# A hybrid encoder on one core: decays of the score matrices moved to later convolutions, a triangular inversion kept on VectorE, two more dense steps before its merge

## The chip, the cores and the metric

The kernel runs on one core of one Trainium2 chip. The metric is the device time of one launch in microseconds; the number given for a kernel is the median of its runs. Lower is better.

## The reference

Two encoder layers over a sequence of 1024 tokens of width 1024, all in float32, and a final RMSNorm. In each layer x is normed, projected by one matrix of 3376 columns, and the columns go to three groups of heads: gated linear attention (GLA), a gated DeltaNet, and cross-attention into 256 memory tokens. The outputs are normed, gated, concatenated and projected back. The change touches the gated DeltaNet and the dense projection alone. For the DeltaNet, q, k and v pass a centred depthwise convolution of 5 taps and SiLU; q and k are L2-normalised. Then, per head, direction and chunk of 64 tokens:

```python
gc = jnp.cumsum(g, axis=-1)
diff = gc[..., :, None] - gc[..., None, :]
decay = jnp.where(incl, jnp.exp(jnp.where(incl, diff, 0.0)), 0.0)
kk = jnp.einsum('bhncd,bhnsd->bhncs', k, k)
a_strict = jnp.where(strict, kk * decay * beta[..., :, None], 0.0)
t_mat = a_strict + jnp.eye(c, dtype=jnp.float32)
sol = lax.linalg.triangular_solve(t_mat, rhs, left_side=True, lower=True, unit_diagonal=True)
qk = jnp.where(incl, jnp.einsum('bhncd,bhnsd->bhncs', q, k) * decay, 0.0)
```

The decays depend on the gates alone, not on q, k or v. The unit triangular matrices of 64 x 64 are inverted once, before the scan over the chunks.

## The kernel before, in words

**Stages.** A layer is `phase_norm` (norm, transposes, the first 432 projection columns, gates), `phase_proj` (the convolutions, L2 norms, decays, score matrices, inversion) and `phase_mix` (the scan over chunks as a chain of blocks, with GLA, attention, gating and the output projection filled in between). TensorE's instructions stay in the order in which the program issues them (`pin`, L92, and `mat`, L97). The instructions of the other engines are placed on each engine by a planner that simulates the program (L1656), apart from those that are pinned too.

**The dense projection.** `dense_gen` (L449) makes the 23 remaining column tiles of 128, each in two halves of 512 tokens. A half is four units of six matmuls of 128x512 (three for each of two k, since float32 is split in a high and a low part). One `next` makes one unit. `pull(ns)` (L475) takes units until ns is used up at 1290 a unit, and `upto(n)` (L482) takes them until n tiles are whole. There are 184 units in a layer, so a unit pulled early is one less later. At the end of a half a sink (L487, L519) copies PSUM out on ScalarE; there are two PSUM buffers (`mm`, L171), so the half after the next waits for it. The weights of the next tile are split at its first unit: `wh` on ScalarE and `wl` on GpSimd (L178).

**The convolutions.** `conv_sink` (L519) for a tile: ScalarE writes `pad` and the middle tap into `acc` (L531, L532); after the second half VectorE adds four taps (L535, 128x1024 each); ScalarE makes the sigmoid in three passes and GpSimd multiplies (L538). `conv_t` (L542) later transposes the result on TensorE. The order of the tiles is three of k, three of v, three of q (L436).

**The decays.** `decays` (L648) is a generator. Its first step builds a mask and issues eight loads of N. Each later step treats one of four heads on 128x1024 elements: a subtraction on GpSimd (L671, pinned), a minimum on VectorE (L672), an exponential on ScalarE (L673). `phase_proj` calls a step after each of the three key convolutions (L599) and after the second and third value convolution (L611); the fifth call finds the generator at its end. The result is first read in `phase_a` (L676), after the query convolutions.

**The inversion.** `invert` (L701) transposes blocks of 32x32 into U (L713) and makes the inverse X column step by column step: for j from 31 down to 1 a product into `tmp` and a subtraction from X. Columns 0 to 29 (`CUT` = 30) are made on VectorE (L732 to L738). The last two columns, in X2, are made by 62 instructions on GpSimd (L724 to L731), and ScalarE copies them into X (L739). Then VectorE transposes X into FT and M for both directions (L745, L747). The merge of the 32-blocks into 64-blocks is matmuls of 32x32 on TensorE (L765, L778). The generator yields how much dense work is to be pulled: 20000 (`INV0`, 16 units), eight single units among the matmuls of the memory's key and value projection (`kv`, L1414 to L1430), and 6000 (`INV`, five units) ahead of the merge.

**The filler.** What is left of the dense units is taken in `phase_mix` by `filler` (L829): 3, 24 and 5 units, then the rest between the steps of the mixers (L860 to L872), and after it the loads and splits of the output weights.

Of the kernel before, what the change touches and what calls it, by code (L numbers as in the profile page):

```python
# [8 lines left out]
F32 = mybir.dt.float32  # L9
# [4 lines left out]
ALU = mybir.AluOpType  # L14
# [3 lines left out]
P = 128  # L18
# [19 lines left out]
LAG = 2  # L38
PRE_D = 24
INV0 = 20000  # L40
INV = 6000
XPOS = 5
DC0 = 0
CUT = 30
MIX0 = 5
MIXU = 21
MIXN = 16
# [12 lines left out]
class Kern:  # L60
# [510 lines left out]
    def phase_proj(self, l):  # L571
        nc = self.nc
        GC, self.closeGC = self.pool("GC", side=self.sb)
        self.ST, self.closeST = self.pool("ST", side=self.sb)
        ST = self.ST
        KTp, closeKT = self.pool("KT", side=self.sb)
        closePX = self.psum(tr=2, cp=2, kv=2)
        dec = self.decays(GC)
        N = next(dec)

        self.kv_d = self.DR.tile([2, NT, P, 384], F32, tag="kvd", name="kv_d")
        self.qd_d = self.DR.tile([2, HD, 4, T], F32, tag="qdd", name="qd_d")
        kT = [KTp.tile([HD, T], F32, name=f"kT{h}") for h in range(4)]
        qT = KTp.tile([HD, 4, T], F32, name="qT")
        tok = lambda: ST.tile([P, NT, 384], F32, tag="tok", name="tok", bufs=1)

        def v_out(i):
            v = ST.tile([P, NT, P], F32, tag="v_t", name="v_t", bufs=1)
            self.conv_t(6 + i, v)
            nc.sync.dma_start(self.kv_d[1, :, :, i * 128:i * 128 + 128].rearrange("t p c -> p t c"), v)  # L590
        U = 1290
        k_tok = tok()
        self.upto(2)
        for i in range(3):

            self.upto(3 + i)
            self.pull(DK * U)
            self.conv_t(3 + i, k_tok[:, :, i * 128:i * 128 + 128])
            if i >= DC0:  # L599
                next(dec, None)  # L600
        self.l2norm(ST, k_tok, 1.0)
        nc.sync.dma_start(self.kv_d[0].rearrange("t p c -> p t c"), k_tok)
        self.upto(6)
        self.pull(DV * U)
        v_out(0)
        q_tok = None
        for i in range(2):
            self.upto(7 + i)
            self.pull(DV * U)
            v_out(1 + i)  # L610
            next(dec, None)  # L611
            if i == 0:
                for h in range(4):
                    self.back_t(k_tok, h, kT[h])
                    self.pull(U)
                q_tok = tok()
        for i in range(3):
            self.upto(9 + i)
            self.pull(DQ * U)
            self.conv_t(i, q_tok[:, :, i * 128:i * 128 + 128])  # L620
        for _ in dec:
            pass
        self.l2norm(ST, q_tok, HD ** -0.5)
        self.pull(8 * U)
        for h in range(4):
            self.back_t(q_tok, h, qT[:, h, :])
            for d in range(2):
                row = ST.tile([P, T], F32, tag="acc", name="row", bufs=3)[0:HD]
                nc.sync.dma_start(row.rearrange("p (t c) -> p t c", t=NT),
                                  self.row_d[:, d * 4 + h].unsqueeze(0).to_broadcast([HD, NT, P]))  # L630
                self.ptt(row, row, qT[:, h, :], ALU.mult)
                nc.sync.dma_start(self.qd_d[d, :, h], row)
            self.pull(U)
        for _ in self.phase_a(N, kT, qT, KTp):
            self.pull(U)
        closeKT()
        self.closeST()
        GQ, self.closeGQ = self.pool("GQ", side=self.sa)
        R, closeR = self.pool("GR", side=self.sa)
        self.gla_gate_ops(l, GQ, R)  # L640
        closeR()
        SX, self.closeSX = self.pool("SX", side=self.sb)
        for g in self.invert(l, N, SX):
            self.pull(g)
        closePX()
# [55 lines left out]
    def invert(self, l, N, SX):  # L701

        nc = self.nc

        U = SX.tile([P, 2, 32, 32], F32, name="U")
# [8 lines left out]
        X = SX.tile([P, 2, 32, 32], F32, name="X")  # L714
        nc.gpsimd.memset(X, 0.0)
        Xf = X.rearrange("p b s c -> p b (s c)")
        nc.gpsimd.memset(Xf[:, :, 0:1024:33], 1.0)

        n2 = 32 - CUT
        X2 = SX.tile([P, 2, 32, n2], F32, name="X2")  # L720
        nc.gpsimd.memset(X2, 0.0)
        for c in range(n2):
            nc.gpsimd.memset(X2[:, :, CUT + c, c:c + 1], 1.0)
        for j in range(31, 0, -1):  # L724
            c0 = max(j - CUT, 0)
            w = n2 - c0
            tmp = SX.tile([P, 2, 32, n2], F32, tag="tmp2", name="tmp2", bufs=1)
            tv = tmp[:, :, 0:j, 0:w]
            sh = [P, 2, j, w]
            self.ptt(tv, U[:, :, 0:j, j:j + 1].to_broadcast(sh), X2[:, :, j:j + 1, c0:].to_broadcast(sh), ALU.mult)  # L730
            self.ptt(X2[:, :, 0:j, c0:], X2[:, :, 0:j, c0:], tv, ALU.subtract)  # L731
        for j in range(CUT - 1, 0, -1):  # L732
            w = CUT - j
            tmp = SX.tile([P, 2, 256], F32, tag="tmp", name="tmp", bufs=1)
            tv = tmp[:, :, 0:j * w].rearrange("p b (s c) -> p b s c", s=j)
            sh = [P, 2, j, w]
            self.tt(tv, U[:, :, 0:j, j:j + 1].to_broadcast(sh), X[:, :, j:j + 1, j:CUT].to_broadcast(sh), ALU.mult)
            self.tt(X[:, :, 0:j, j:CUT], X[:, :, 0:j, j:CUT], tv, ALU.subtract)  # L738
        self.act(X[:, :, :, CUT:], X2)  # L739

        FT = [SX.tile([P, 4, NT, 32], F32, name=f"FT{d}") for d in range(2)]
        fl = lambda v: v.rearrange("p h t c -> p (h t) c")
# [9 lines left out]
        for c in kv:  # L752
            yield c
        yield INV
        for g in range(2):
# [904 lines left out]
```

## Time and profile before

| | us |
|---|---|
| median of three runs (1391.15 to 1397.26) | 1391.71 |
| the profiled execution's own time | 1387.57 |
| its span from first to last instruction | 1385.8 |

The mean granted TensorE clock of the profiled execution is 0.965 of full speed. 1.77 us of its time lie around the span. Windows and timelines are in microseconds from the start of the span. PE is TensorE's matmuls, DVE VectorE, ACT ScalarE, POOL GpSimd. A matmul's duration overlaps the next one's, so starts are compared, not durations. The name behind `<-` in square brackets is what ended the idle time before the instruction. A line can be a helper's: L84 is any ScalarE activation, L87 a VectorE and L90 a GpSimd two-input operation, L98 a matmul.

### The profile page before, as it was taken

What the parts mean: (1) busy time and instruction counts of PE and PEld (TensorE: products, weight loads), DVE (VectorE), ACT (ScalarE), POOL (GpSimd) and SP (SyncE); (2) the same over time, 40 slices, a digit from 0 to 9 for tenths busy, and PEclk for the clock granted to TensorE, in tenths of its full rate; (3) what the DMA queues carried; (4) which work ended last, traced back from release to release, by engine and by line L of the source; (5) the groups of instructions that cost most, each with busy time, mean ns of one, the idle gap of its engine ahead of it and who ended that gap; (6) DMA issues with size and microseconds to landing.
All of it is one profiled execution on the core that took longest, in us unless ns stands there. A gap on an engine that the chain in (4) does not pass through costs nothing. (4 is left out here: it accounts for less than half of the span.)

```text
span 1385.8 us, 24239 instructions
## 1 busy us (share of the span) xinstructions
PE 1260.7 (91%) x9482; PEld 1047.5 (76%) x9482; DVE 814.8 (59%) x1163; ACT 655.5 (47%) x1373; POOL 549.6 (40%) x579
## 2 busy tenths in 40 slices
PE   6998799987999988999999988996978998999997
PEld 5986688776777777887788766884767787778886
DVE  5336855498377557356272578455865784564553
ACT  5335564162766655233262545531637675543432
POOL 4026434576534544211310454444854445432111
PEclk9999999999999999999999999998999999999999
DMA  7161234752686865244652413257427776642532
GB/s 223 57 134 35 74 91 130 245 157 69 187 242 197 236 192 144 81 145 125 188 169 66 107 46 106 61 158 221 136 66 225 210 229 203 205 130 80 161 103 106
DMA packets 247857, 198.99 MB, mean 144 GB/s; under 512 B 68032, under 2 KB 215936, under 8 KB 247744
## 3 DMA queue, kind: packets, MB, share of 16 engines
q1 hardware_dynamic: 245584, 189.59, 47.2%
q10 hardware_dynamic: 2016, 7.34, 1.5%
q8 instruction: 75, 1.23, 0.4%
q0 software_dynamic: 144, 0.52, 0.1%
q14 instruction: 38, 0.31, 0.1%
HBM read 138.82 MB, written 58.59 MB: 142 GB/s over the span
## 5 line engine op out<-in xcount | busy, mean ns | idle before, releaser
L98 PE MATMUL mm<-Hh,wh 128*128 128x512 f32 x736 | 311.8, 424 | 31.7 <-ACT acc L84 15.9
L98 PE MATMUL mm<-Hh,wl 128*128 128x512 f32 x736 | 295.9, 402 | 0.0
L98 PE MATMUL mm<-Hl,wh 128*128 128x512 f32 x736 | 295.6, 402 | 0.0
L90 POOL TENSOR_TENSOR wl<-wr,wh 128x1024 fp32r<-128x1024 f32 x46 | 119.4, 2596 | 211.0 <-ACT wh L84 188.3
L98 PEld LDWEIGHTS mm<-Hh,wh 128*128 128x128 f32 x736 | 143.5, 195 | 66.7 <-ACT acc L84 19.3
L535 DVE SCALAR_TENSOR_TENSOR acc<-pad,convw,acc 128x1024 f32<-128x1024 f32 x72 | 139.9, 1943 | 66.4 <-ACT acc L84 63.8
L98 PEld LDWEIGHTS mm<-Hh,wl 128*128 128x128 f32 x736 | 143.2, 195 | 32.3
L98 PE MATMUL mm<-wo,oh 128*128 128x512 f32 x512 | 167.1, 407 | 0.2 <-DVE xr L87 0.2
L98 PEld LDWEIGHTS mm<-Hl,wh 128*128 128x128 f32 x736 | 144.2, 196 | 26.0
L90 POOL TENSOR_TENSOR ol<-z,oh 128x512 fp32r<-128x512 f32 x32 | 41.2, 1286 | 163.6 <-ACT oh L84 161.4
L98 PEld LDWEIGHTS mm<-wo,oh 128*128 128x128 f32 x512 | 90.3, 189 | 17.8 <-issue 0.8
L98 PE MATMUL mm<-wo,ol 128*128 128x512 f32 x256 | 101.2, 395 | 0.0
L90 POOL TENSOR_TENSOR S<-S,dec 96x384 f32<-96x384 f32 x56 | 55.5, 991 | 87.4 <-DVE S L87 66.9
L90 POOL TENSOR_TENSOR acc<-acc,pad 128x1024 f32<-128x1024 f32 x18 | 45.6, 2531 | 107.8 <-ACT pad L84 107.8
L84 ACT ACTIVATE wh<-wr 128x1024 fp32r<-128x1024 f32 x46 | 48.4, 1053 | 74.8 <-PE mm L98 66.2
L98 PEld LDWEIGHTS cp<-S,wq 96*128 96x128 f32 x480 | 62.7, 197 | 14.9 <-ACT oa L84 6.4
L98 PE MATMUL cp<-S,wq 96*128 96x96 f32 x480 | 65.1, 280 | 9.2 <-ACT oa L84 5.5
L84 ACT ACTIVATE oh<-z 128x512 fp32r<-128x512 f32 x32 | 20.2, 632 | 80.4 <-DVE z L87 80.3
L87 DVE TENSOR_TENSOR vn<-u,cp 64x384 f32<-64x384 f32 x60 | 33.0, 550 | 40.9 <-PE cp L98 33.4
L98 PEld LDWEIGHTS mm<-wo,ol 128*128 128x128 f32 x256 | 48.1, 188 | 11.5
L90 POOL TENSOR_TENSOR sp<-sp,sg 128x512 f32<-128x512 f32 x32 | 45.3, 1417 | 28.8 <-ACT sg L84 17.6
L90 POOL TENSOR_TENSOR row<-row,qT 96x1024 f32<-96x1024 f32 x16 | 38.0, 2383 | 44.0 <-DMA row<-row_d 29.3
(311 smaller groups left out, 2652.1 us busy)
## 6 DMA issues: line engine op xcount, KB each, us to landing
wr<-in_w_in_dram SPq DMA_DIRECT2D x46, 512.0 KB, 4.0
kv<-kv_d SPq DMA_DIRECT2D x32, 384.0 KB, 4.4
zT<-sp SPq DMA_DIRECT2D x32, 256.0 KB, 2.4
ge_d<-qe SPq DMA_DIRECT2D x32, 256.0 KB, 3.7
wor<-in_w_out_dram SPq DMA_DIRECT2D x16, 512.0 KB, 4.6
gqk<-ge_d SPq DMA_DIRECT2D x16, 512.0 KB, 4.0
z<-zT SPq DMA_DIRECT2D x16, 512.0 KB, 4.5
row<-row_d SPq DMA_DIRECT2D x16, 384.0 KB, 6.3
```

Of the source, the lines that this page charges most:

```text
L84: return self.nc.scalar.activation(out, in_, func, **kw)
L87: return self.nc.vector.tensor_tensor(out, a, b, op=op)
L90: return self.nc.gpsimd.tensor_tensor(out, a, b, op=op)
L98: return self.pin(self.nc.tensor.matmul(*args, **kw))
L535: nc.vector.scalar_tensor_tensor(acc, pad[:, j:j + T], self.convw[:, f, j:j + 1], acc, op0=ALU.mult, op1=ALU.add)
```

## The change

The decay steps are no longer called after the key convolutions. They are called after the second and third value convolution (heads 0 and 1) and after the first two query convolutions (heads 2 and 3; the last call ends the generator). The first step with its eight loads stays where it is. In the inversion all 32 columns are made on VectorE, in 62 instructions in place of 58; X2, its memsets, the 62 GpSimd instructions and ScalarE's copy go. `INV` is 9000, seven units in place of five.

```diff
-INV = 6000
+INV = 9000
 XPOS = 5
-DC0 = 0
-CUT = 30
...
             self.conv_t(3 + i, k_tok[:, :, i * 128:i * 128 + 128])
-            if i >= DC0:
-                next(dec, None)
...
             self.conv_t(i, q_tok[:, :, i * 128:i * 128 + 128])
-        for _ in dec:
-            pass
+            next(dec, None)
...
-        n2 = 32 - CUT
-        X2 = SX.tile([P, 2, 32, n2], F32, name="X2")
-        nc.gpsimd.memset(X2, 0.0)
-        for c in range(n2):
-            nc.gpsimd.memset(X2[:, :, CUT + c, c:c + 1], 1.0)
         for j in range(31, 0, -1):
-            c0 = max(j - CUT, 0)
-            w = n2 - c0
-            tmp = SX.tile([P, 2, 32, n2], F32, tag="tmp2", name="tmp2", bufs=1)
-            tv = tmp[:, :, 0:j, 0:w]
-            sh = [P, 2, j, w]
-            self.ptt(tv, U[:, :, 0:j, j:j + 1].to_broadcast(sh), X2[:, :, j:j + 1, c0:].to_broadcast(sh), ALU.mult)
-            self.ptt(X2[:, :, 0:j, c0:], X2[:, :, 0:j, c0:], tv, ALU.subtract)
-        for j in range(CUT - 1, 0, -1):
-            w = CUT - j
+            w = 32 - j
...
-            self.tt(tv, U[:, :, 0:j, j:j + 1].to_broadcast(sh), X[:, :, j:j + 1, j:CUT].to_broadcast(sh), ALU.mult)
-            self.tt(X[:, :, 0:j, j:CUT], X[:, :, 0:j, j:CUT], tv, ALU.subtract)
-        self.act(X[:, :, :, CUT:], X2)
+            self.tt(tv, U[:, :, 0:j, j:j + 1].to_broadcast(sh), X[:, :, j:j + 1, j:].to_broadcast(sh), ALU.mult)
+            self.tt(X[:, :, 0:j, j:], X[:, :, 0:j, j:], tv, ALU.subtract)
```

## Rows read from the trace of the kernel before

**Rows 1.** Page, part 1: busy us, share of the span, instructions.
```profile
PE 1260.7 (91%) x9482; PEld 1047.5 (76%) x9482; DVE 814.8 (59%) x1163; ACT 655.5 (47%) x1373; POOL 549.6 (40%) x579
```

**Rows 2.** Waits of PE, whole span: us in total, times, longest.
```profile
PE mm L98 <- ACT acc L84: 15.9, 8, 3.5
```

**Rows 3.** Windows, busy us of each engine: value to query convolutions; second layer's mix.
```profile
180.00:240.00 60.00, 60.00 (x300) 50.21 (x299) 34.76 (x29) 31.93 (x49) 23.33 (x15) 1.00 0.36 95
...
1050.00:1240.00 190.00, 175.04 (x1530) 148.18 (x1529) 120.94 (x214) 115.58 (x261) 83.94 (x84) 0.96 0.70 203
```

**Rows 4.** Timeline of PE, first layer's convolutions: start, us, instruction [idle before].
```profile
117.44 0.50 PE L98 MATMUL mm<-Hh,wh 128*128 128x512 f32 x1 [1.54 <-ACT acc L84]
...
133.06 0.80 PE L98 MATMUL mm<-Hh,wh 128*128 128x512 f32 x1 [3.50 <-ACT acc L84]
...
139.70 0.39 PE L98 MATMUL mm<-Hh,wl 128*128 128x512 f32 x1
...
223.38 1.03 PE L101 MATMUL tr<-ident,acc 128*128 128x128 f32 x8
```

**Rows 5.** Timeline of DVE, first layer's convolutions: the four taps.
```profile
117.42 8.87 DVE L535 SCALAR_TENSOR_TENSOR acc<-pad,convw,acc 128x1024 f32<-128x1024 f32 x4 [3.97 <-ACT acc L84]
...
148.42 5.75 DVE L535 SCALAR_TENSOR_TENSOR acc<-pad,convw,acc 128x1024 f32<-128x1024 f32 x2 [1.05 <-ACT acc L84]
...
159.34 1.27 DVE L535 SCALAR_TENSOR_TENSOR acc<-pad,convw,acc 128x1024 f32<-128x1024 f32 x1
...
195.66 7.50 DVE L535 SCALAR_TENSOR_TENSOR acc<-pad,convw,acc 128x1024 f32<-128x1024 f32 x4 [0.43 <-ACT acc L84]
...
208.71 7.50 DVE L535 SCALAR_TENSOR_TENSOR acc<-pad,convw,acc 128x1024 f32<-128x1024 f32 x4 [4.94 <-ACT acc L84]
```

**Rows 6.** Timeline of POOL, first layer's convolutions.
```profile
117.28 2.41 POOL L90 TENSOR_TENSOR wl<-wr,wh 128x1024 fp32r<-128x1024 f32 x1
...
119.71 2.86 POOL L90 TENSOR_TENSOR N<-N,gB 128x1024 f32<-128x1024 f32 x1
...
219.79 2.40 POOL L90 TENSOR_TENSOR acc<-acc,pad 128x1024 f32<-128x1024 f32 x1 [7.38 <-ACT pad L84]
```

**Rows 7.** Timeline of ACT, first layer's convolutions.
```profile
128.54 1.04 ACT L84 ACTIVATE N<-N 128x1024 f32<-128x1024 f32 x1
```

**Rows 8.** Windows of tile X, first layer's inversion: DVE, ACT, POOL busy (count).
```profile
283.80:328.80 45.00, 38.36 (x59) 0.33 (x1) 27.51 (x62) 0.96 0.35 109
```

**Rows 9.** Timeline of DVE, first layer's inversion.
```profile
299.78 2.66 DVE L87 TENSOR_TENSOR X<-X,tmp 128x400 f32<-128x400 f32 x1
...
305.85 1.57 DVE L87 TENSOR_TENSOR X<-X,tmp 128x442 f32<-128x442 f32 x1
...
309.52 0.63 DVE L87 TENSOR_TENSOR X<-X,tmp 128x450 f32<-128x450 f32 x1
...
325.27 0.22 DVE L87 TENSOR_TENSOR X<-X,tmp 128x58 f32<-128x58 f32 x1
328.74 1.97 DVE L745 STREAM_TRANSPOSE FT<-X 128x1024 f32<-128x1024 f32 x1 [3.25 <-ACT X L84]
```

**Rows 10.** Timeline of POOL, first layer's inversion.
```profile
299.28 2.73 POOL L90 TENSOR_TENSOR wl<-wr,wh 128x1024 fp32r<-128x1024 f32 x1
...
334.64 2.37 POOL L90 TENSOR_TENSOR wl<-wr,wh 128x1024 fp32r<-128x1024 f32 x1
```

**Rows 11.** Timeline of ACT, first layer's inversion.
```profile
328.38 0.33 ACT L84 ACTIVATE X<-X 128x128 f32<-128x128 f32 x1 [15.84 <-POOL X L90]
```

**Rows 12.** Timeline of PE, first layer's inversion.
```profile
322.01 0.59 PE L98 MATMUL mm<-Hh,wh 128*128 128x512 f32 x1
...
328.82 0.39 PE L98 MATMUL mm<-Hh,wl 128*128 128x512 f32 x1
331.21 0.50 PE L98 MATMUL mm<-Hh,wh 128*128 128x512 f32 x1 [2.00 <-ACT sg L84]
...
338.55 1.92 PE L98 MATMUL cp<-FT,N 32*32 32x32 f32 x124 [5.50 <-DVE FT L745]
```

## The prediction, made before the change was run

> **What bounds the kernel now.** I read the page's busy times first: TensorE is busy for 91% of the span, 125 us are not [rows 1]. Its matmuls stay in program order, so each of these gaps moves all that comes after it. The list of TensorE's waits then says which gaps the change can reach. The longest in total is for ScalarE to empty a PSUM buffer in the convolutions, 15.9 us in eight waits [rows 2]; the longest in the inversion is the merge's for VectorE's transpose FT, 5.50 in the first layer [rows 12]. The table of windows says where there is room: in the later convolutions of the first layer TensorE is busy for all 60.00 us, with VectorE at 34.76 and GpSimd at 23.33 [rows 3]. Last come the timelines of the two places, the convolutions [rows 4 to 7] and the inversion [rows 9 to 12]. The second layer repeats the first there, so I price one layer and double it.
>
> **Decays leave the key convolutions.** Per layer three heads move: 0, 1 and 2, which after the change stand behind later convolutions as heads 1, 2 and 3. The fourth stays at the second value convolution. What moves is a GpSimd subtraction of 2.86 us, a VectorE minimum, a ScalarE exponential of 1.04 us [rows 6, 7] and no DMA: the eight loads are issued by the first step, which stays, so SP's queue sees nothing. On GpSimd a subtraction passes the convolutions' products and the weight splits between its old place and its new one.
> A convolution is a loop: its four taps on VectorE, the sigmoid on ScalarE, then ScalarE empties the next half, and only then do the next taps start. Without a decay the loop takes 208.71 - 195.66 = 13.05 us. With decays the second and third starts lie at 117.42 and, after two loops, 148.42, so 15.5 us a loop [rows 5]. I see two causes: the taps take 8.87 us in place of 7.50, as they meet a subtraction besides a weight split [rows 5, 6], so 1.37; and the exponential stands on ScalarE ahead of the emptying, 1.04 [rows 7]. The sum is 2.4 a head, which fits.
> Taken out, the start at 117.42 comes 1.54 earlier, for as long as TensorE waited there [rows 4], at 115.9, and two loops of 13.05 later stands 142.0 in place of 148.42. **Gain: 6.4 us** a layer. TensorE, whose work in a loop is eight dense units and a group of transposes (8 x 1.41, worked out below, and 1.03 [rows 4]: 12.3 us), still waits in each loop, but less than the 3.50 of the row at 133.06 [rows 4].
>
> **Decays arrive in the later convolutions.** There the same three heads make the loops late by at most 3 x 2.4 = 7.2 us, and by the key convolutions' own measure 6.4. Two meet in one loop, behind the last value and the first query convolution. Behind GpSimd's subtractions its products and weight splits queue; behind the exponentials ScalarE's emptying of PSUM, for which TensorE waits. The place where it shows last is the transposes of the last query convolution: its GpSimd product ends at 219.79 + 2.40 = 222.19, TensorE takes it at 223.38 [rows 4, 6], so 1.2 us of lateness are covered. No dense work stands behind them that could go first. The cost of a wait there lies between 0 (the planner puts the pieces into the idle time of rows 3) and 7.2 - 1.2 = 6.0. I take 6.4 - 1.2 = 5.2, from the nearest row, the same instructions in the same kind of loop.
> After a wait of this size the clock is low for a while: behind the 3.50 at 133.06 the granted clock falls, and 18 dense matmuls start over 6.64 us, while 30 at the full clock start over 6.81 [rows 4, 12]. That is 6.64 - 17 x 0.235 = 2.6 us, and I add it. In the key convolutions that loss was hidden in the loop's 15.5 us, so it is not gained there. **Net of the decays: -6.4 + 5.2 + 2.6 = +1.4** a layer, between -6.4 and +2.2.
>
> **The inversion, on VectorE alone.** Instructions without company take 0.22 us for 58 elements and 0.63 for 450 [rows 9], so 0.16 us and 1.05 ns an element. Before, 58 of them have 17980 elements, 28.1 us. After, 62 have 21824: 32.8 us and 0.1 for the gaps, **+4.8**. Busy in the row are 38.36 - 0.06 of the first transpose = 38.3 [rows 8]; 10.2 more than 28.1. Two of the instructions meet a weight split (299.78: 2.66 in place of 0.58, under the split from 299.28 [rows 9, 10]) and five a sink's product (305.85: 1.57 in place of 0.62 [rows 9]): 2 x 2.1 + 5 x 0.95 = 9.0. The remaining 1.1 or so comes from the company of the two columns' instructions. That goes: **-1.1**. So does the wait of 3.25 for ScalarE's copy [rows 9]: **-3.25**. X is ready 0.4 us later than before.
> But ScalarE's copy, which stood 15.84 us in front of ScalarE's other work [rows 11], held back the emptying of the `kv` buffers, the next `wh` and with it the split at 334.64 [rows 10], which ran under the transposes, where it cost nothing. Without the copy this split and one sink's product come some ten microseconds earlier, behind the last `kv` matmuls at 322 [rows 12], inside VectorE's longer chain: 2.1 as at 299.78 and about 1 more. X is ready at 328.74 + 3.5 = 332.2, and the merge's FT 3.5 later than 338.55. The stall of 2.00 on `sg` [rows 12] goes, since ScalarE is free, but TensorE then only waits longer for FT: 8 units behind the last `kv` matmuls, from 322.01 at 6 x 0.235 = 1.41 each, end at 333.3, and FT comes at 342. The two units more are 2.8 us that the filler has no longer to do; in the mix TensorE is busy for 175 of 190 us [rows 3], so I count all of it. For a wait of 8.7 us in one piece the clock costs a little more than after 5.50 and 2.00: I add 0.4, from a bound of 0 and the 2.6 above. **Net: +3.5 - 2.8 + 0.4 = +1.1** a layer, between 0.4 - 2.8 = -2.4 (no new meeting with GpSimd) and +3.5 + 2.6 = +6.1 (the mix, bound by its chain there, gives nothing back).
> The memsets of X2 and the 62 GpSimd instructions lie beside other work and count nothing more: GpSimd's own end was seen only through the copy.
>
> **A rule weighed.** The 62 GpSimd instructions are busy for 27.51 us beside VectorE's, and yet cost VectorE 1.1 us [rows 8, 9]; a 2.7 us split costs it 2.1 [rows 9, 10]. The Trainium skill, page "SBUF — State Buffer", section "Who interferes with whom", says that a VectorE instruction with two SBUF inputs and a GpSimd instruction that reads SBUF exclude each other for the whole instruction, and that the order of issue decides who waits. By it the short ones would make VectorE wait as well as the long, up to 27.51 us in all, and the chain would come out much shorter without them; the row says they do not, the long ones agree, and the sum goes by the rows.
>
> **Sum.** 2 x (1.4 + 1.1) = +5.0 us. The profiled execution would go from 1387.57 (span 1385.8 and 1.77 around it) to 1392.6. That execution is 4.1 under the median of the three runs, 1391.71, so the median becomes **1396.7 us**. A measurement of this kernel tells 0.5%, 7.0 us, from no change; this is 0.36%.
>
> **Rivals.** *The later convolutions hide the decays* (faster). For it: 60.00 of 60.00 us of TensorE without a wait, VectorE 42% idle [rows 3]. Against: the loop is 13.05 against TensorE's 12.3, its slack was gathered earlier and is used up at the last transposes, to 1.2. Then 2 x (-6.4 + 1.1) = -10.6: 1381.1.
> *A subtraction holds VectorE for its whole length* (slower). Place: the loop of the first query convolution, where two of them follow a weight split. In the key convolutions a subtraction cost the taps 1.37 of its 2.86, but a weight split, 2.41 long, costs the taps at 195.66 all of its length (7.50 against four times 1.27, as at 159.34) [rows 5, 6]. Three heads at 2.86 - 1.37 = 1.5 more are +4.5 a layer: 2 x (2.5 + 4.5) = +14: 1405.7. It decides once the taps of that loop take over 10.3 us (7.50 and twice 1.37). The skill's rule above is this rival's rule too.
> *The inversion meets no new GpSimd work* (no change to tell): if the planner puts the split behind VectorE's chain, -2.4 in place of +1.1, 2 x (1.4 - 2.4) = -2: 1389.7.
> *The change does not do what it says*: only the subtraction is pinned; the planner may place the rest of a decay, or the subtraction, where little meets it, and both sides of the move vanish: 2 x 1.1: 1393.9.
>
> **How the numbers follow.** My forecast 0.42, hidden decays 0.13, held VectorE 0.22, inversion without company 0.14, move without effect 0.09. Faster by over 0.5%: 0.13 and 0.01 of the forecast's spread. Slower: 0.22 and 0.13 of the forecast's, whose +5.0 stands close to the limit of 7.0. Same: 0.51. The range reaches from near the hidden decays, 1383, to past the held VectorE, 1407; it leaves out most of the fastest case and both unknown ends at once.
>
> **What would show it.** Right: the waits at 117.44 and 133.06 shrink to under 2 us; a new wait of TensorE for GpSimd's `acc` ahead of the last query transposes, some 5 us long; taps of about 10 us in the loop of two decays; FT's first transpose straight behind the last subtraction, with a weight split inside the chain; `kv` emptied at once; the merge's wait near 9 us in one piece. Wrong: the later convolutions still at 60 of 60; the merge's wait no longer than 5.5 us; a mix that takes as long as before in spite of two units less.

## The result and the profile after

The changed kernel takes 1405.25 us (median), 1.0100 times the kernel before, with a 95% interval of 1.0082 to 1.0119: slower by 14 us. Forecast were +5.0 us and a median of 1396.7; the time lies inside the range, near its upper end, and the outcome that was given most of the chance, a change of less than 0.5%, is not the one that came. The profiled execution after is 1405.37 us long, its span 1403.7, against 1387.57 and 1385.8. Line numbers fall by two in the convolutions (L98 is now L96, L87 L85, L535 L533) and by up to twenty in the inversion (L745 is L725).

The busy times of the page, part 1, answer to [rows 1]. GpSimd has 59 us less to do and VectorE 12.6 more. TensorE is busy 6.3 us longer with the same 9482 matmuls; the mean granted clock of the execution is 0.956, where it was 0.965:

```profile
PE 1267.0 (90%) x9482; PEld 1054.6 (75%) x9482; DVE 827.4 (59%) x1171; ACT 654.4 (47%) x1371; POOL 490.5 (35%) x449
```

In the list of TensorE's waits (total us, times, longest) the row of [rows 2] has lost 6.3 us, and a wait of 9.0 us, one in each layer, is new at the head of the list. The waits for FT are now up to 7.4 us:

```profile
PE tr L99 <- POOL acc L88: 24.0, 4, 9.0
PE cp L96 <- DVE FT L725: 18.1, 4, 7.4
...
PE mm L96 <- ACT acc L82: 9.6, 6, 2.5
```

The window of the later convolutions, for [rows 3], shows the new wait as 9 us of missing TensorE time. The granted clock is 0.91 over the window and 0.67 in the ten microseconds that hold the end of the wait (column before the last two), where it was 1.00:

```profile
180.00:240.00 60.00, 51.00 (x242) 42.34 (x242) 35.17 (x25) 30.40 (x46) 27.48 (x13) 0.91 0.32 82
...
220.00:230.00 10.00, 6.63 (x27) 5.75 (x28) 3.94 (x5) 4.79 (x10) 3.31 (x2) 0.67 0.42 122
```

TensorE's timeline, for [rows 4 and 12]: smaller waits in the key convolutions, the transposes of the last query convolution late, the merge's wait for FT in two pieces, and a pause in its second half for which the profile has no releaser (the last section comes back to it):

```profile
127.17 0.50 PE L96 MATMUL mm<-Hh,wh 128*128 128x512 f32 x1 [1.15 <-ACT acc L82]
...
141.24 0.71 PE L96 MATMUL mm<-Hh,wh 128*128 128x512 f32 x1 [1.99 <-ACT acc L82]
...
223.37 1.97 PE L99 MATMUL tr<-ident,acc 128*128 128x128 f32 x8 [9.00 <-POOL acc L88]
...
333.66 0.25 PE L96 MATMUL cp<-FT,N 32*32 32x32 f32 x4 [1.80 <-DVE FT L725]
341.28 1.92 PE L96 MATMUL cp<-FT,N 32*32 32x32 f32 x124 [7.37 <-DVE FT L725]
...
355.46 0.32 PE L96 MATMUL cp<-FT,N 32*32 32x32 f32 x13 [2.65 <-issue]
```

Before, that pause stood at the last of these matmuls and was shorter:

```profile
350.86 0.21 PE L98 MATMUL cp<-FT,N 32*32 32x32 f32 x1 [0.60 <-issue]
```

VectorE's timeline of the last two query convolutions answers to the last rows of [rows 5]. One decay's minimum (`N<-N,cap`) stands between the taps of the second query convolution, and two decays meet the last one: that takes 12.4 us from the first tap to the end of the fourth, where it took 7.5:

```profile
186.34 7.74 DVE L533 SCALAR_TENSOR_TENSOR acc<-pad,convw,acc 128x1024 f32<-128x1024 f32 x3 [0.43 <-ACT acc L82]
194.00 1.22 DVE L85 TENSOR_TENSOR N<-N,cap 128x1024 f32<-128x1024 f32 x1
195.13 1.28 DVE L533 SCALAR_TENSOR_TENSOR acc<-pad,convw,acc 128x1024 f32<-128x1024 f32 x1
...
201.88 4.40 DVE L533 SCALAR_TENSOR_TENSOR acc<-pad,convw,acc 128x1024 f32<-128x1024 f32 x2 [4.87 <-ACT acc L82]
206.21 3.41 DVE L85 TENSOR_TENSOR N<-N,cap 128x1024 f32<-128x1024 f32 x1
209.54 2.95 DVE L533 SCALAR_TENSOR_TENSOR acc<-pad,convw,acc 128x1024 f32<-128x1024 f32 x1
212.42 0.68 DVE L113 COPY tok<-tr 128x512 f32<-128x512 f32 x1
213.02 1.27 DVE L533 SCALAR_TENSOR_TENSOR acc<-pad,convw,acc 128x1024 f32<-128x1024 f32 x1
214.21 1.21 DVE L85 TENSOR_TENSOR N<-N,cap 128x1024 f32<-128x1024 f32 x1
```

GpSimd's timeline beside it (for [rows 6]). The last product, for which TensorE waits, comes behind a weight split:

```profile
202.28 2.92 POOL L88 TENSOR_TENSOR N<-N,gB 128x1024 f32<-128x1024 f32 x1
205.17 3.37 POOL L88 TENSOR_TENSOR wl<-wr,wh 128x1024 fp32r<-128x1024 f32 x1
208.50 2.91 POOL L88 TENSOR_TENSOR N<-N,gB 128x1024 f32<-128x1024 f32 x1
218.67 2.35 POOL L88 TENSOR_TENSOR wl<-wr,wh 128x1024 fp32r<-128x1024 f32 x1 [7.25 <-ACT wh L82]
220.97 2.34 POOL L88 TENSOR_TENSOR acc<-acc,pad 128x1024 f32<-128x1024 f32 x1
```

Before, the product of 219.79 in [rows 6] was ahead of that split:

```profile
222.15 2.38 POOL L90 TENSOR_TENSOR wl<-wr,wh 128x1024 fp32r<-128x1024 f32 x1
```

On ScalarE a decay's exponential and the copy `wh` now stand ahead of the last of the sigmoid's three passes:

```profile
216.55 1.04 ACT L82 ACTIVATE N<-N 128x1024 f32<-128x1024 f32 x1
217.50 1.04 ACT L82 ACTIVATE wh<-wr 128x1024 fp32r<-128x1024 f32 x1
218.44 1.04 ACT L82 ACTIVATE pad<-pad 128x1024 f32<-128x1024 f32 x1
```

And the inversion on VectorE, for [rows 8 and 9]: the window of tile X (DVE, POOL busy), the one instruction of the chain's end that meets a split (its row on GpSimd stands last), and FT straight behind the last subtraction:

```profile
284.30:331.60 47.30, 43.77 (x62) 0.00 (x0) 1.00 0.41 125
```

```profile
323.66 2.61 DVE L85 TENSOR_TENSOR tmp<-U,X 128x350 f32<-128x350 f32 x1
326.31 0.52 DVE L85 TENSOR_TENSOR X<-X,tmp 128x350 f32<-128x350 f32 x1
...
331.35 0.22 DVE L85 TENSOR_TENSOR X<-X,tmp 128x62 f32<-128x62 f32 x1
331.61 1.91 DVE L725 STREAM_TRANSPOSE FT<-X 128x1024 f32<-128x1024 f32 x1
```

```profile
323.27 2.63 POOL L88 TENSOR_TENSOR wl<-wr,wh 128x1024 fp32r<-128x1024 f32 x1 [15.98 <-ACT wh L82]
```

**Stages.** From the profiled executions of the two kernels and of the runs below I took the starts of the same TensorE instructions: the transposes of the first, sixth and ninth convolution, the end of the merge, the end of the layer. Their differences, in us, layer 0 / layer 1:

```
run                   conv 1 to 6    conv 6 to 9    conv 9 to merge end   mix
before                85.4 / 83.9    29.9 / 29.9    133.2 / 142.9         332.2 / 342.4
before, again         84.3 / 84.9    29.9 / 30.0    133.3 / 143.5         336.7 / 342.9
the change            77.9 / 77.4    39.2 / 39.2    139.3 / 145.9         334.2 / 344.7
decays alone          77.3 / 77.9    39.2 / 39.2    135.2 / 143.8         336.0 / 352.9
decays alone, again   78.6 / 78.5    39.2 / 39.2    136.4 / 147.1         333.3 / 345.5
columns and units     85.1 / 84.5    29.9 / 30.0    137.2 / 146.4         337.1 / 337.3
columns alone         84.3 / 85.8    29.9 / 30.0    135.4 / 146.0         339.2 / 343.2
columns alone, again  84.3 / 83.8    29.9 / 30.0    135.1 / 145.5         332.4 / 342.9
units alone           85.8 / 84.7    29.9 / 30.0    134.3 / 141.8         337.2 / 340.1
one decay a loop      80.1 / 79.9    36.6 / 36.6    136.0 / 145.2         329.1 / 343.9
subtract on VectorE   78.7 / 77.5    37.1 / 37.8    137.4 / 147.6         333.9 / 341.8
decays behind taps    78.9 / 77.2    29.9 / 30.0    133.0 / 143.9         332.9 / 344.0
the same, inversion   77.5 / 77.8    29.9 / 30.0    135.6 / 148.3         344.2 / 341.8
```

In the three pairs of profiles of one kernel the convolutions repeat to 1 or 2 us, the merge to 3.3 or better, a mix only to some 7. So the first two columns carry conclusions from a single profile, the mix carries none. For the change the first three columns add up, against the mean of the two profiles of the kernel before, to +8.4 us in layer 0 and +4.9 in layer 1: 13 of the 14 us lie ahead of the mixes.

### The profile page after: what moved, and what is told of

Read it like the earlier page. It is cut to its first block, busy times and chain, and to the rows that moved or that the text cites. A ratio compares the mean times of both kernels' runs of the same rounds, so it can differ in the third digit from the quotient of the medians.

```text
span 1403.7 us, 24128 instructions
## 1 busy us (share of the span) xinstructions
PE 1267.0 (90%) x9482; PEld 1054.6 (75%) x9482; DVE 827.4 (59%) x1171; ACT 654.4 (47%) x1371; POOL 490.5 (35%) x449
## 4 chain that ended last, share of the span: by engine, by line
PE 44%; DVE 22%; DMA 12%; ACT 11%; issue 5%; POOL 2%; SPq 2%; DVEq 0%; ACTq 0%; POOLq 0%
PE mm L96 28%; DVE acc L533 7%; PE cp L96 4%; DVE tmp L85 3%; ACT pad L82 3%; PE tr L99 3%; DVE X L85 3%; DMA qd_d<-row 3%; DMA wor<-in_w_out_dram 2%; PE pt L96 2%; PE R L96 2%; PE x L96 2%; ACT ge L82 2%; PE gb L96 1%; DMA s_d<-sb 1%
## 5 line engine op out<-in xcount | busy, mean ns | idle before, releaser
L96 PE MATMUL mm<-Hh,wh 128*128 128x512 f32 x736 | 309.3, 420 | 18.2 <-ACT acc L82 9.6
L96 PE MATMUL mm<-Hh,wl 128*128 128x512 f32 x736 | 294.0, 399 | 0.0
L96 PE MATMUL mm<-Hl,wh 128*128 128x512 f32 x736 | 293.8, 399 | 0.0
L88 POOL TENSOR_TENSOR wl<-wr,wh 128x1024 fp32r<-128x1024 f32 x46 | 116.2, 2526 | 241.7 <-ACT wh L82 234.9
L96 PEld LDWEIGHTS mm<-Hh,wh 128*128 128x128 f32 x736 | 143.0, 194 | 51.5 <-ACT acc L82 12.4
L533 DVE SCALAR_TENSOR_TENSOR acc<-pad,convw,acc 128x1024 f32<-128x1024 f32 x72 | 133.5, 1857 | 70.1 <-ACT acc L82 67.5
L96 PE MATMUL mm<-wo,oh 128*128 128x512 f32 x512 | 167.3, 408 | 0.0
L96 PEld LDWEIGHTS mm<-Hh,wl 128*128 128x128 f32 x736 | 142.1, 193 | 31.8
L96 PEld LDWEIGHTS mm<-Hl,wh 128*128 128x128 f32 x736 | 143.3, 195 | 26.1
L96 PEld LDWEIGHTS mm<-wo,oh 128*128 128x128 f32 x512 | 90.2, 189 | 18.1 <-issue 0.6
L96 PE MATMUL mm<-wo,ol 128*128 128x512 f32 x256 | 101.2, 395 | 0.0
L88 POOL TENSOR_TENSOR acc<-acc,pad 128x1024 f32<-128x1024 f32 x18 | 44.9, 2494 | 114.0 <-ACT pad L82 114.0
L96 PEld LDWEIGHTS cp<-S,wq 96*128 96x128 f32 x480 | 63.5, 199 | 16.8 <-ACT oa L82 12.0
L96 PE MATMUL cp<-S,wq 96*128 96x96 f32 x480 | 65.7, 282 | 10.9 <-ACT oa L82 9.6
L96 PEld LDWEIGHTS mm<-wo,ol 128*128 128x128 f32 x256 | 48.1, 188 | 11.4
L85 DVE TENSOR_TENSOR vn<-u,cp 64x384 f32<-64x384 f32 x60 | 33.0, 550 | 39.1 <-PE cp L96 24.3
L96 PEld LDWEIGHTS R<-vn,kend 64*96 64x96 f32 x448 | 43.4, 165 | 16.1 <-issue 10.0
```

The lines of the kernel that those rows point to most:

```text
L85: return self.nc.vector.tensor_tensor(out, a, b, op=op)
L88: return self.nc.gpsimd.tensor_tensor(out, a, b, op=op)
L96: return self.pin(self.nc.tensor.matmul(*args, **kw))
L533: nc.vector.scalar_tensor_tensor(acc, pad[:, j:j + T], self.convw[:, f, j:j + 1], acc, op0=ALU.mult, op1=ALU.add)
```

## Experiments

**Decays alone.** The kernel before, with the decays moved as in the change:

```diff
             self.conv_t(3 + i, k_tok[:, :, i * 128:i * 128 + 128])
-            if i >= DC0:
-                next(dec, None)
...
             self.conv_t(i, q_tok[:, :, i * 128:i * 128 + 128])
-        for _ in dec:
-            pass
+            next(dec, None)
```

> The kernel before with the decays moved as in the change, inversion and its dense units as before. Theory (the later convs give back what the key convs gain, the inversion is the larger part): about +6 us, near 1397 (1394 to 1401): key and value convs about 9 us shorter in layer 0 and 5 to 6.5 in layer 1, a TensorE wait of about 9 us at the last query transposes of each layer, layer 0 even at the end of its scores (-0.6) and layer 1 some 7 behind. Rival 1 (the inversion carries it all): 1391 within 3 us, the wait at the last query transposes under 6 us. Rival 2 (the decays carry it all, and what follows the scores is only phase): 1402 to 1407.

Measured: 1400.4 us, ratio 1.0091 (1.0055 to 1.0126). The waits are those expected, 9.00 us in layer 0 and 8.99 in layer 1; the decays alone cost 8 us by the medians and 13 by the ratio, at the upper end of the theory or above it. Rival 1 falls with this; the next run decides on rival 2.

**All of the inversion, without the decays.** The changed kernel with the decays back at the key convolutions (the first edit above, reversed).

> The changed kernel with the decays put back beside the key convs: all columns on VectorE and the larger number of dense units are left. Theory: +8 to +12 us, near 1400: the merge ends 5 to 6 us later in layer 0, and the mix, with two dense units less to fill it, does not get shorter. Rival 1 (the forecast's own terms: +1.1 a layer): 1393.5. Rival 2 (the decays carry it all): 1391 within 2 us.

Measured: 1398.5, ratio 1.0060 (1.0038 to 1.0081). So the inversion costs 6 (medians) to 8 us (ratio), three to four times the forecast's 2.2, and neither part carries the change alone. The cost is at the lower edge of the theory's, the place fits only in part: from the ninth convolution to the end of the merge it is 4.0 us more in layer 0, not 5 to 6. Together the two make 15 us by the medians and 21 by the ratios, with some 5 of uncertainty; the change has 14.

**Two dense units alone.** `INV = 6000` to `9000`, in the kernel before.

> The kernel before with only the number of dense units ahead of the merge changed (9000 in place of 6000: two units more). TensorE waited 5.50 us there for FT, so two units (2.8 us) fit into the wait. Theory (the mix does not give the two units back): 1391 within 2 us, the wait for FT 2.8 us shorter and the mix 2 to 3 us longer than its own work less. Rival (the mix is filled by dense work that is now done, so it is shorter by it): -2.8 a layer, near 1386.

Measured: 1389.5, ratio 0.9989 (0.9961 to 1.0018). In layer 0 TensorE waits 3.07 us for FT in place of 5.50. The interval nearly reaches the rival's -5.6 us, so this run leans to the theory without settling it; the next one does more.

**Columns alone.** All columns on VectorE, `INV = 6000` kept:

```diff
...
-        for j in range(CUT - 1, 0, -1):
-            w = CUT - j
+        for j in range(31, 0, -1):
+            w = 32 - j
...
```

> The kernel before with all columns on VectorE and nothing else (dense units as before, decays as before). Theory (the columns carry the inversion's half, the two units nothing): 1397 to 1402, FT 3 to 5 us later, TensorE waiting 7 to 10 us for it. Rival (the forecast's term: chain +0.4, split and product inside it 3.1): FT no more than 3.5 us later in each layer and the mix unchanged, 1392 to 1398. Second rival (nothing, the split waits elsewhere): 1389 to 1392.

Measured: 1399.1, ratio 1.0056 (1.0033 to 1.0079), against 1.0060 with the two units. With intervals of some 3 us on either side, nothing shows that the units give anything back. The time is the first theory's, but its reason is not quite: the chain from the first column to FT takes 47.1 us in layer 0 and 52.2 in layer 1, against 44.9 and 50.2 before: 2.0 to 2.2 longer, not 3 to 5, which is the first rival's size, though the time lies above that rival's. TensorE's wait for FT in layer 0 is 4.53 + 7.27 = 11.8 us.

**Columns, the kernel before, and decays, a second time.** The same kernels once more, for second profiles.

> The run with the columns alone once more, for a second profiled execution. Theory (the columns cost at the merge: FT 2 to 3 us later after the chain's start, and the merge behind a longer TensorE wait): from the last product of the scores to the end of the merge 1 to 4 us more than before in each layer, the mix as long as before within its own scatter (329 to 339 us in layer 0 in the profiles so far). Rival (the 8 us lie in the mix): both mixes 3 us or more longer than in the kernel before of the same call.

> The kernel before once more, for a second profiled execution on the same chip. From it the scatter of each stage between two executions of one program: stages ahead of the mix within 1 us, the mix of a layer within 10 us.

> The run with the decays alone once more, for a second profiled execution. Theory (nothing gained among the convolutions, and the slow clock behind the long wait): from the start of a layer to the end of its scores 0 to 6 us more than before in each layer, wait at the last query transposes 9 us; the 11 us that the first profile showed in the mix of layer 1 are scatter and do not come again. Rival (they belong to the change): again 8 us or more.

Measured, in one execution each: 1389.9, 1391.0 and 1404.2; the first is below all twelve earlier times of the columns (1392.2 to 1403.6), so a single time tells little here. The rows "again" of the table above are theirs. Columns: conv 9 to merge end +1.8 to +2.2 in layer 0 and +2.0 to +3.1 in layer 1, in both profiles; the mix of layer 0 was 339.2 once and 332.4 the other time, so those 7 us were scatter. The stages thus show 4 to 5 us of the columns' cost; where the rest of the 8 lies is open. Decays: the 352.9 of the mix of layer 1 did not come again, and were scatter too; what does come again is 39.2 where 29.9 stood, and the wait of 9.0. From the start of a layer to the end of its scores that profile is 1 to 3 us above the two of the kernel before in layer 0, as expected, and 6 to 9 in layer 1, where 0 to 6 were expected. The expectation of 1 us for the stages ahead of the mix holds for the kernel before; in the pairs of the other two it was too narrow, for the merge by most.

**One decay in each loop.** Inversion as before; the decays stand behind the first, second and third value transposes and the first query transposes, one step earlier than in the change, so that no loop should hold two:

```diff
         v_out(0)
+        next(dec, None)
...
             self.conv_t(i, q_tok[:, :, i * 128:i * 128 + 128])
-        for _ in dec:
-            pass
+            if i == 0:
+                next(dec, None)
```

> The kernel before with the decays behind the first, second and third value transposes and the first query transposes: one step earlier than in the change, so that the loop of the last query conv holds one subtraction and one minimum and not two. Inversion as before. Theory (it is the second decay in the last loop that makes the 9 us wait): the key convs keep most of the gain (6 to 9 us a layer), the wait at the last query transposes falls under 3 us; 1375 to 1383. Rival (any decay in these loops puts its minimum between the taps and the chain behind it, so the wait stays at 5 us or more): 1388 to 1397.

Measured: 1399.3, ratio 1.0060 (1.0032 to 1.0088). The theory missed; the rival's wait came, and the time lies above the range of either. With a single subtraction in the last loop TensorE still waits:

```profile
223.17 1.12 PE L101 MATMUL tr<-ident,acc 128*128 128x128 f32 x4 [6.37 <-POOL acc L90]
```

VectorE's rows say why. The minimum stands between the taps again, and meets the weight split that GpSimd began at 207.59 for 3.38 us; its 1.22 us become 3.42:

```profile
204.30 4.41 DVE L535 SCALAR_TENSOR_TENSOR acc<-pad,convw,acc 128x1024 f32<-128x1024 f32 x2 [4.88 <-ACT acc L84]
208.63 3.42 DVE L87 TENSOR_TENSOR N<-N,cap 128x1024 f32<-128x1024 f32 x1
211.97 1.27 DVE L535 SCALAR_TENSOR_TENSOR acc<-pad,convw,acc 128x1024 f32<-128x1024 f32 x1
```

What follows: taps, sigmoid and the ScalarE copies of the next half are one chain through all nine convolutions. A decay inside it delays every later step. From the first to the last convolution's transposes layer 0 takes 116.6 to 117.9 us in the four profiles with the decays moved so far (the change, decays alone twice, this run), against 115.3 and 114.2 in the kernel before: the key convolutions' gain was handed on, and 1 to 4 us were lost besides. That is read from rows here; the run with the decays behind the taps, below, tests it.

**Subtraction on VectorE.** The changed kernel with `self.tt` for `self.ptt` in the decays.

> The changed kernel with the subtraction of the decays on VectorE, in place of GpSimd, at the same four places. Theory (the chain is only lengthened: 1.2 us of subtraction on VectorE stands for the 1.4 to 1.5 us that a GpSimd subtraction takes from the taps): no change, 1405 within 4 us, wait at the last query transposes 7.5 to 10 us. Rival (GpSimd holding VectorE, and the splits queued behind it, made the wait): the wait falls to 5 us or less, 1394 to 1398.

Measured: 1398.5, ratio to the kernel before 1.0055 (1.0028 to 1.0082), about 6 us faster than the change. Time and wait come within 0.5 us of the rival's ranges and outside the theory's, so GpSimd's part matters. Two rows of TensorE show that the wait shrank and moved up by one convolution; at the last transposes there is none:

```profile
208.37 1.97 PE L99 MATMUL tr<-ident,acc 128*128 128x128 f32 x8 [5.10 <-POOL acc L88]
...
222.07 1.03 PE L99 MATMUL tr<-ident,acc 128*128 128x128 f32 x8
```

The 5.10 us are again a product behind a split on GpSimd (split at 202.69, product at 205.00). The planner's order changed with the edit, so the price of the subtraction and the order are not told apart by this run.

**GpSimd in the written order.** To test the order alone, the changed kernel's products and splits were pinned to the order of the program:

```diff
-        self.ptt(lo, raw, hi.bitcast(F32), ALU.subtract)
+        self.pin(self.ptt(lo, raw, hi.bitcast(F32), ALU.subtract))
...
-                self.ptt(acc, acc, pad[:, 0:T], ALU.mult)
+                self.pin(self.ptt(acc, acc, pad[:, 0:T], ALU.mult))
```

> The changed kernel with GpSimd's conv products and weight splits kept in the order in which they are written: the product of the last query conv ahead of the next split, and the fourth subtraction behind that product too. Theory (of the 9.0 us, about 3.3 us are the split and its ScalarE copy that went ahead of the last product, 2.4 us the second decay in the last loop): wait at the last query transposes 2 to 4.5 us, 5 us a layer less, 1393 to 1399. Rival (the order on GpSimd is only where a wait shows; the chain through the taps sets it): wait 6 us or more, 1400 to 1406.

Measured: 1459.3, ratio 1.0507 (1.0464 to 1.0550). A miss that says nothing of its question: every split now queues behind a product that waits for taps and sigmoid, and the next matmuls wait for the split, as here in the value convolutions:

```profile
179.53 0.80 PE L96 MATMUL mm<-Hh,wl 128*128 128x512 f32 x1 [11.69 <-POOL wl L88]
```

What the order alone is worth was not measured by itself; the written order as a whole costs 70 us.

**Decays behind the taps.** The kernel before without any decay among the convolutions: two right behind the taps of the last query convolution, two between the back-transposes, subtraction on VectorE and pinned there:

```diff
...
-            if i >= DC0:
-                next(dec, None)
...
             v_out(1 + i)
-            next(dec, None)
...
+            if i == 2:
+                next(dec)
+                next(dec)
             self.conv_t(i, q_tok[:, :, i * 128:i * 128 + 128])
...
             self.back_t(q_tok, h, qT[:, h, :])
+            if h % 2:
+                next(dec)
...
-            self.pin(self.ptt(r, r, gcs.unsqueeze(3).to_broadcast(bshape), ALU.subtract))
+            self.pin(self.tt(r, r, gcs.unsqueeze(3).to_broadcast(bshape), ALU.subtract))
```

> The kernel before with no decay among the convolutions: two heads right behind the taps of the last query conv, two behind the second and fourth head of the query back-transposes, the subtraction on VectorE; inversion as before. Theory (taps, sigmoid and the ScalarE copies of the next conv form one chain through all nine convs, so that a decay costs its 2.4 us wherever it stands inside, and the last query transposes came at 222.5 to 223.4 us in all four placements so far): outside that chain the last query transposes of layer 0 come at 214 to 216 us, with less than 1 us of wait, and the time falls by 10 to 18 us, to 1374 to 1382. Rival (what comes behind, the norm of the queries on VectorE and the row products, is then late by as much): query back-transposes at 233 us or later in layer 0, 1388 to 1394.

Measured: 1380.5, ratio 0.9929 (0.9904 to 0.9955): 10 us faster than the kernel before, 25 faster than the change. TensorE has no wait at the last query transposes, the taps are 7.5 us again, and the two decays fill VectorE's idle time behind them:

```profile
202.65 7.49 DVE L535 SCALAR_TENSOR_TENSOR acc<-pad,convw,acc 128x1024 f32<-128x1024 f32 x4 [4.94 <-ACT acc L84]
210.05 0.69 DVE L115 COPY tok<-tr 128x512 f32<-128x512 f32 x1
210.65 1.22 DVE L87 TENSOR_TENSOR N<-N,gB 128x1024 f32<-128x1024 f32 x1
211.91 1.23 DVE L87 TENSOR_TENSOR N<-N,cap 128x1024 f32<-128x1024 f32 x1
213.05 1.22 DVE L87 TENSOR_TENSOR N<-N,gB 128x1024 f32<-128x1024 f32 x1
214.30 3.31 DVE L87 TENSOR_TENSOR N<-N,cap 128x1024 f32<-128x1024 f32 x1
```

The transposes come at 217.28, not at 214 to 216, since this execution reached the first convolution 2.3 us later than most of the others; from there it is 108.8 us against 115.3 and 114.2 in the two profiles of the kernel before. The queries' back-transposes are at 229.1 in place of 235.2, so the rival falls: what comes behind was not late.

**The same, with the change's inversion.** The changed kernel with its decays placed as in the run before.

> The changed kernel with the decays placed as in the run with the decays behind the taps: only its inversion (all columns on VectorE, two dense units more) is left of the change. Theory (the inversion costs its 8 us by itself, whatever the decays do): 1386 to 1391, 8 us above that run; the last step of the inversion's chain 2 to 3 us later after its start than with two columns on GpSimd. Rival (the two parts only cost together): 1380 to 1383.

Measured: 1383.4, ratio 0.9964 (0.9938 to 0.9989). The chain to FT is 47.7 us, against 44.9 in the run before, as expected. In time the inversion costs 0.9964 / 0.9929, 5 us, here; with intervals of 3.5 us on either side that settles neither the theory's 8 nor the rival's 0. By this run together with the two of the columns, 1.0060 and 1.0056, the inversion as before is the better one.

This kernel and the one with the subtraction on VectorE differ in the places of the decays alone: 0.9964 against 1.0055. So the placement by itself, with the same engines and the same inversion, is worth some 13 us.

## Why the prediction was right in sign and short in size

**Key convolutions, -6.4 a layer.** Right: over conv 1 to 6 the means of the three profiles with the moved decays are 6.9 and 6.7 us under those of the six with the decays in their old place (84.9 / 84.6 against 78.0 / 77.9). The two waits of [rows 4] are down to 1.15 and 1.99.

**Later convolutions, +5.2.** This step failed. The place of the wait and its releaser were as forecast, though the two decays met in the loop of the last query convolution, one later than the text had it. But the wait is 9.0, and conv 6 to 9 takes 9.3 us more in each layer, above the bound of 6.0 that the text gave. I had priced a decay by the key convolutions' average, 6.4 for three. The rows show what the sum is made of. One of the three decays makes the taps of the second query convolution 10.1 us long in place of 7.5, +2.6. The two others make those of the last 12.4, +4.9. And from the last tap to the end of the product it takes 214.29 to 223.31, 9.0 us, where it took 216.21 to 222.19, 6.0: +3.0, because the planner put an exponential and `wh` ahead of the sigmoid's last pass, and the split of 2.35 us ahead of the product. 2.6 + 4.9 + 3.0 less the slack of 1.2 is 9.3; TensorE waited 9.0. The price of 2.4 a head was about right (2.5); what was left out is the order behind the taps. That it is worth 3.0 is read from rows, not from a run of its own; rows of other runs agree. From the last tap to the end of the product it takes 8.1 us with one decay in each loop, where `wh` and the split also went first, and 6.0 and 6.4 with the subtraction on VectorE and with the decays behind the taps, where the product went ahead of the split.

**Clock, +2.6.** Right in kind, too large by 1 us: behind the wait of 9.00 us the slow transposes at 223.37 take 1.97 us for 1.03 (the granted clock from 223.4 to 226 is 0.50, the lower of its two levels), and from them to the queries' back-transposes it is 13.4 us in place of 11.8, so 1.6. How much of it lasts is not shown: to the end of the scores the change takes 42.7 / 51.2 us from there, the kernel before 43.3 / 48.8 once and 45.1 / 50.5 the other time. Net, the decays cost +2.4 and +2.6 in conv 1 to 9 of the two layers and, in the mean of the two profiles with the decays alone, +2.6 and +2.2 from there to the end of the merge: about +10 for the forecast's +2.8, with 8 to 13 measured.

**Inversion, FT +3.5.** The mechanism was right, one piece was not. 43.77 us are busy: 32.8 without company, 9.0 for the same two splits and five products as before, 2.1 for the third split, at 323.27, which does stand inside the chain as the text said, make 43.9. But the sink's product comes at 337.35, behind it; without its 1 us the forecast is +2.5, and +2.3 was measured (284.35 to 331.61 is 47.3, before 44.9). FT's second transpose came at 339.1 and let TensorE go on at 341.28; the forecast was 342.0. ScalarE's copy and the wait of 3.25 are gone, `kv` is emptied at once, the merge waits 1.80 + 7.37 = 9.2 (forecast 8.7).

**The mix gives the two units back, -2.8.** This step failed too, as far as the runs tell. I counted all of it because TensorE was busy for 175 of 190 us there. By the ratios the two units make the kernel 0.6 us slower with all columns on VectorE (1.0060 against 1.0056) and 1.5 faster without (0.9989), each with some 3 us of uncertainty or more; 5.6 faster were forecast. Part of them is lost in the merge of layer 0: its second half holds the pause at 355.46, 2.65 us, and pauses of 1.6 to 2.1 us in the other three runs with columns and units and of 1.76 with the units alone, against 0.3 to 1.2 without the units. What the rest runs into in the mix is below its scatter, and stays open.

**The rivals.** The time is the one of the rival in which a subtraction holds VectorE, 1405.7, but its reason holds only in part, so that the match is luck. It is in part luck, too, that the time lies in the range, which was drawn to reach past that rival: forecast were +2.8 for the decays and +2.2 for the inversion, and the runs show about +10 and 6 to 8. Its point of decision was taps of over 10.3 us in the loop with two decays: they are 8.6 by themselves (4.40 + 2.95 + 1.27) and 12.0 with the minimum among them. A meeting with a subtraction costs them 1.7 to 1.9 us, between the forecast's 1.4 and the rival's 2.9; moving the subtraction to VectorE gave 6 of the 14 us back. The rest is order, and the inversion, which that rival left at the forecast's +1.1. Hidden decays fell with the 51.00 us of the window. The inversion did meet new GpSimd work. The moves were made; the planner put two of the three minima at the worst place, among the taps.

**The rule weighed.** Rows of long instructions agree with the Trainium skill, page "SBUF — State Buffer", section "Who interferes with whom", that such a pair excludes each other. The minimum at 206.21 ends 1.08 us after the split from 205.17 (208.54 to 209.62), the tap at 209.54 ends 1.08 after the subtraction at 208.50 (211.41 to 212.49): about their own length, so both seem to have begun only when GpSimd was done. For the short ones the window of tile X decided rightly: with the 62 GpSimd instructions gone the sum above closes to 0.1 us, so that they had cost VectorE the 1.1 of the forecast and nothing near their 27.51 us.

## What to carry to other kernels

Moving work along a chain that is itself the bound only moves the wait: follow the chain (here taps, sigmoid, copy, next taps) through all its steps, and look for a place behind its end, not for idle engine time inside it. When a planner sets the order, price an edit with the new instruction at the worst place that its inputs allow, and pin it behind the last instruction that something waits for. Do not count a filler that is taken ahead as time saved from busy shares alone: here TensorE was busy for 175 of 190 us in the stage that the two units left, and no saving shows beyond the scatter.

## What was not expected of the hardware

A GpSimd subtraction of this form takes 1.93 us in a row beside which VectorE stands idle (at 226.02 in the run with the pinned order) and 2.72 to 2.94 where VectorE is at work, so both sides seem to pay for a meeting.

The pause without a releaser stands at one place of TensorE's program. In all fourteen profiles it comes, in layer 0, behind 4034 of its matmuls and weight loads; the two units more put 12 matmuls ahead of it, so that it falls on the 116th of the merge's 128 matmuls in place of the last one (on the 119th in the run with the pinned order). And in every profile it ends 1.2 to 1.5 us after a packet of DMA queue q8, which the page lists as carrying instructions. That points to the arrival of TensorE's code and not to another engine's work. Why it is longer with the units (1.6 to 2.65 us; 0.5 in the run with the pinned order) is open.

Layer 1 reached its first convolution 98.5 to 101.0 us after its start in the change and in the two profiles with the decays alone, against 97.6 to 98.3 in the six with the decays in their old place; nothing in the edit touches that stretch, and it stays open.
